# Three projection columns taken half by half, and layer 1's tables stored from ACT's queue

## The chip, the cores and the metric

The kernel runs on one core of one Trainium2 chip. The metric is the device time of one execution in microseconds (us). The engines of the core are TensorE (PE, with its weight loads as PEld), VectorE (DVE), ScalarE (ACT), GpSimd (POOL) and SyncE (SP). Each executes its own instruction list strictly in order. SP, ACT and POOL can also issue DMAs, and a DMA waits at its place in the list of the engine that issues it.

## The reference

A two-layer encoder on x of 1024 tokens by 1024 channels, in float32. Cut to what matters:

```python
for l in range(2):
    u = x @ w_in[l]                       # 1024 -> 2048: 16 columns of 128 channels
    conv, hyena, s5, q, k, v = split(u)   # 4 mixer groups of 256 channels
    # q, k: RMS norm per head, 2-D rotary (rope), then attention with 4 query and 2 key heads
    # hyena: 3-tap conv, then two long convolutions, by spectra of filters made from a small MLP
    # s5: linear state space, run both ways with tables made from lambda, B, C
    # conv: a * sigmoid(gate), 31 taps, layer norm, silu
    x = layernorm(ALPHA * x + concat(rms(each group)) @ w_out[l])
    x = layernorm(ALPHA * x + moe(x))     # 16 experts, each takes 128 tokens, SwiGLU
```

The hyena spectra and the s5 tables of a layer depend on weights alone, not on x.

## The kernel before, in words

**Projection.** `mixer(l)` loads the rows of the layer, normalises them (layer 1) and transposes them on PE into two resident tiles, `hTh` (high part) and `hTl` (rest). Each of 16 columns of `w_in` is then taken by `col(ct, evac)` (L1043): two PSUM tiles (one per half of the tokens), two weight loads `wr` of half a column on SP's queue, the cast `wh` on ACT (L1053), the rest `wl` on POOL (L1054), and 48 matmuls of 128x128 by 128x512: 8 blocks of the contraction, 2 halves, 3 products. A half needs only the transposed rows of its own 512 tokens. 16 columns are 768 matmuls a layer. The parts run in the order `qkv` (columns 12 to 15), `gated`, `chunks`, `hyrows` in layer 0, and `qkv`, `hyrows`, `gated`, `chunks` in layer 1. In `qkv` columns 12 to 14 are evacuated into `uq`, transposed into `rx`, and put through `rope` (L760 to L790) on DVE and POOL; column 15 goes to `VD`.

**The side work.** `s5_setup` and `spectra` make the tables of a layer. For layer 0 they run beside layer 0's projection (`side` in `mixer`), all of them emitted ahead of the parts (`step(side, 40)`). The four quarters of `s5_setup` compute `Q` and `R` (in a buffer with the tag `M`) on POOL, `M` on DVE, transposes of `M` and products `Q,Bb` on PE, and `Kp` on DVE, which empties the PSUM of `Q,Bb` (L589 to L592). `spectra` makes four `gf` and four `Z` (the DVE functions `stage1` and `fly`, L275 to L307). For layer 1 both run beside layer 0's experts (`experts`, L1420), where `Q` and `R` are on DVE too.

**Experts.** Weights stream in as `er`; ACT casts `eh` (L1460), DVE subtracts `el` (L1463), PE multiplies; POOL gathers each expert's rows (`xs`, L1488) and scatters the result (`accD`, L1538).

**What sets the order.** The code is emitted once; a list scheduler of the build with a time model then fixes each engine's instruction list. PSUM has pairs of banks with names; `ps(tag)` looks up which bank names a tag may use and takes them in turn. A tag that is not listed falls back to `acc` (L172), and in layer 0's mixer that is so for the tag `su` of `s5_setup`. Tiles of one bank name are handed out in the order in which they are emitted, two at a time.

Of the kernel before, what the change touches and what calls it, by code (L numbers as in the profile page):

```python
# [11 lines left out]
F32 = mybir.dt.float32  # L12
F32R = mybir.dt.float32r
# [123 lines left out]
class Trunk:  # L137
# [178 lines left out]
    def spectra(self, l, side, HD, after=None):  # L316

        nc, I = self.nc, self.I
        with self.pool("sh", 1, side) as hp:
            hid = hp.tile([128, 512], F32, tag="hid2", name=self.name("hid"))  # L320
            with self.pool("ml", 1, side) as mp:
# [8 lines left out]
                for s, dst in enumerate((h1, hid)):  # L330
                    arg = mp.tile([128, 512], F32, tag="harg", name=self.name("arg"))
                    red = mp.tile([128, 512], F32, tag="hred", name=self.name("red"))
                    p = self.ps(tag="hy")
                    for h in range(2):
                        r = slice(64 * h, 64 * h + 64)
# [8 lines left out]
            with self.pool("sp", 1, side) as sp:  # L344
                dft_s = self.const("dft_s", [128, 8, 128], pool=sp)
                w3r = I["hw3"][l].rearrange("p (o s f c) -> p o s f c", o=2, s=2, f=2)
                for f in range(2):
                    c = slice(128 * f, 128 * f + 128)
                    win = sp.tile([128, 8, 128], F32, tag="win", name=self.name("win"))
                    nc.sync.dma_start(win, I["hy_win"][:, :, c])  # L350
                    for o in range(2):
                        w3 = sp.tile([128, 2, 128], F32, tag="w3", name=self.name("w3"))
                        nc.sync.dma_start(w3, w3r[:, o, :, f])
                        hb = sp.tile([1, 128], F32, tag="hb", name=self.name("hb"))
                        nc.sync.dma_start(hb, I["hbias"][l, o:o + 1, c])
                        gf = sp.tile([128, 8, 2, 128], F32, tag="gf", bufs=2 if l else 1, name=self.name("gf"))
                        for i in range(0, 8, 2):
                            p = self.ps((128, 2, 2, 128), tag="hy")
                            for j in range(2):
                                r = slice(64 * (i // 4), 64 * (i // 4) + 64)  # L360
                                n = 128 * ((i + j) % 4)
                                self.mm(p[:, j], hid[r, n:n + 128], w3[r], True, True)
                            nc.vector.tensor_mul(gf[:, i:i + 2], p, win[:, i:i + 2, None].to_broadcast([128, 2, 2, 128]))
                        nc.vector.memset(gf[0:1, 0, 1], 0.0)
                        nc.vector.tensor_add(gf[0:1, 0, 0], gf[0:1, 0, 0], hb)
                        yield

                        def emit(p, r):
                            q = (8 - r) % 8
                            self.mm(p[:, 0, :], self.dft_f[:, r, 0, :], gf[:, r, 0, :], True, False)  # L370
                            self.mm(p[:, 0, :], self.dft_f[:, q, 0, :], gf[:, q, 1, :], False, True)
                            self.mm(p[:, 1, :], self.dft_f[:, r, 1, :], gf[:, r, 0, :], True, False)
                            self.mm(p[:, 1, :], dft_s[:, q, :], gf[:, q, 1, :], False, True)

                        A = sp.tile([128, 4, 2, 128], F32, tag="A", name=self.name("A"))
                        B = sp.tile([128, 4, 2, 128], F32, tag="B", name=self.name("B"))
                        self.stage1(sp, emit, A, B, 128)
                        if l:
                            yield
                        Z = sp.tile([128, 8, 2, 128], F32, tag="gf", bufs=2 if l else 1, name=self.name("Z"))  # L380
                        self.fly(sp, A, B, Z, 128)
                        yield
                        (nc.sync if l == 0 else nc.gpsimd).dma_start(HD[o, f], Z)
                        yield


# [2 lines left out]
    def s5_setup(self, l, side, dram, after=None, between=()):  # L389
        nc, I = self.nc, self.I  # L390
        SD, KD, rD = dram
        v = nc.vector
        gp = nc.gpsimd
        q_ = nc.sync if l == 0 else gp
        with self.pool("s5q", 1, side) as keep, ExitStack() as work:
            sp = work.enter_context(self.pool("s5p", 1, side))

# [80 lines left out]
            u = t([2, 16], "u8")  # L478
# [56 lines left out]
            for q in range(4):  # L535
# [30 lines left out]
                for k in range(2):  # L566
                    p = self.ps((128, 4, 128), tag="su")
# [6 lines left out]
                hi = [tables[1][:, c, gs, :, None].to_broadcast([128] + sh) for c in range(2)]  # L574
                lo = [tables[0][:, c, gs, None, :].to_broadcast([128] + sh) for c in range(2)]
# [4 lines left out]
                for gi in range(4):  # L580
                    g = 4 * q + gi
                    for d in range(2):
                        o = pk[d][32 * gi:32 * gi + 32]
                        h = slice(64 * d, 64 * d + 64)
                        w = slice(2 * d, 2 * d + 8)
# [411 lines left out]
    def mixer(self, l, setup, st):  # L997
# [5 lines left out]
        with ExitStack() as ph:  # L1003
# [43 lines left out]
            def col(ct, evac):  # L1047
                ps = [self.ps(tag="col") for _ in range(2)]
                for k0 in (0, 4):
                    raw, wh, wl = [ww.tile([128, 4, 128], t, tag=n, bufs=b, name=self.name(n))  # L1050
                                   for t, n, b in zip((F32, F32R, F32R), ("wr", "wh", "wl"), (2, 2, 4))]
                    nc.sync.dma_start(raw, I["w_in"][l, ct, :, k0:k0 + 4])
                    nc.scalar.copy(wh, raw)  # L1053
                    nc.gpsimd.tensor_sub(wl, raw, wh.bitcast(F32))  # L1054
                    for f in range(2):
                        r = slice(512 * f, 512 * f + 512)
                        for k in range(4):
                            self.mm3(ps[f], wh[:, k, :], wl[:, k, :], hi[:, k0 + k, r], lo[:, k0 + k, r], k0 + k == 0, k0 + k == 7)
                for f in range(2):
                    evac(f, ps[f].rearrange("p (i n) -> p i n", n=128))  # L1060

            def rows(a, f):
                u = wp.tile([128, 10, 128], F32, tag="hyu", bufs=2, name=self.name("hyu"))
                col(4 + 2 * a + f, lambda f, p: nc.scalar.copy(u[:, 1 + 4 * f:5 + 4 * f], p))
                v.memset(u[:, 0, 0:1], 0.0)
                v.memset(u[:, 9, 127:128], 0.0)
                v.tensor_copy(u[:, 0, 1:128], u[:, 8, 0:127])
                v.tensor_copy(u[:, 9, 0:127], u[:, 1, 1:128])
                d = hz.tile([128, 8, 128], F32, tag="hx" if a else "hz", bufs=4 if a else 2, name=self.name("hx"))
                self.hyena_short(l, u, sw, 2 * a + f, d, wp)  # L1070
                xs.append(d)
# [16 lines left out]
                    step(n0, 1)  # L1088

            def qkv():  # L1090
                for c in range(4):
                    u = wp.tile([128, 8, 128], F32, tag="hyu", bufs=2, name=self.name("uq"))
                    col(12 + c, lambda f, p: nc.scalar.copy(u[:, 4 * f:4 * f + 4], p))
                    x = a0.tile([128, 8, 128], F32, tag="aQ100" if c % 2 else "aQ202", name=self.name("rx"))
                    for i0 in (0, 4):
                        p = self.ps((128, 4, 128), tag="tp")
                        for i in range(4):
                            self.tr(p[:, i, :], u[:, i0 + i, :])
                        nc.scalar.copy(x[:, i0:i0 + 4], p)
                    if c < 3:  # L1100
                        self.rope(c, x, tab, gn[:, c // 2], RD, a0)
                    else:
                        nc.sync.dma_start(VD, x)
                    yield
                ready.append(1)
# [435 lines left out]
    def run(self, depth=DEPTH):  # L1541
        nc, tc = self.nc, self.tc
        self.rt = self.ctx.enter_context(tc.tile_pool(name="rt", bufs=1))
        setup = self.setup(0)
        for l in range(depth):
            self.psum(mm="mm", hy="hy", tp="tp", cv="cv", tx="cv tp", acc="acc", col="mm")
            with ExitStack() as st:
                mg, ws, hz = self.mixer(l, setup, st)
                self.psum(mm="mm acc", tp="tp cv", tx="tp cv", acc="hy")
                lg = self.project(l, mg, ws, hz)  # L1550
            sl = self.route(l, lg)
            self.psum(mm="mm acc", tp="tp", tx="tp", hy="cv", su="hy")
            side = iter(())
            if l + 1 < depth:
                setup = self.setup(l + 1)
                side = chain(self.s5_setup(l + 1, "right", setup[1]), self.spectra(l + 1, "right", setup[0]))
            self.experts(l, sl, side, *((5, 4) if l + 1 < depth else (10, 0)))
            for _ in side:
                pass
        with self.pool("fin", 2) as pool:  # L1560
            dst = self.out.rearrange("(n i) d -> i n d", i=8)
            for i, h in enumerate(self.rows_in(depth, pool, 2, 4)):
                nc.scalar.dma_start(dst[i], h)
# [20 lines left out]
```

## Time and profile before

| | |
|---|---|
| three runs | 2885.1, 2892.15, 2893.3 us, median 2892.15 us |
| the profiled execution | 2887.34 us, span 2885.2 us |
| granted TensorE clock, mean | 0.917 |
| busy in the span | PE 85%, DVE 79%, ACT 46%, POOL 20% |
| layer 0's projection | ends at about 346 us of the span |
| layer 0's experts | about 855 to 1533 us |
| layer 1's projection | about 1558 to 1831 us |

The span is that of one execution taken by the profiler; its own time is 2.1 us longer, and it lies 4.8 us under the median. "Busy" counts compute instructions, not waits, and is an average over stages with different limits.

### The profile page before, as it was taken

To read this page: it belongs to the slowest core of one execution; us is meant where nothing else is said; L and a number is where in the kernel's file an instruction comes from. 1 tells how busy PE (TensorE), PEld (TensorE's weight loads), DVE (VectorE), ACT (ScalarE), POOL (GpSimd) and SP (SyncE) were. 2 spreads that over 40 slices of the span, in tenths; PEclk is the share of its full clock that TensorE was granted. 3 is DMA by queue.
4 is the path that set the end of the run, shared out by engine and by line. 5 is a ranking of instruction groups with operands and counts; after the bars stand their busy time and mean duration, and the time that the engine had idled before them with its cause. 6 is when DMAs were issued, how large, how long until landed. Compare 5 with 4: busy or idle time off the path is not lost.

```text
span 2885.2 us, 32858 instructions
## 1 busy us (share of the span) xinstructions
PE 2461.9 (85%) x12054; PEld 1911.1 (66%) x12054; DVE 2271.7 (79%) x3635; ACT 1321.6 (46%) x1471; POOL 574.5 (20%) x376
## 2 busy tenths in 40 slices
PE   3889968879949978999994999789995899999992
PEld 2668734657738756778883787456684788777781
DVE  8984877677659989998886578687666799888886
ACT  2212313333128755666662332323411677766772
POOL 2663110312021022210102422112201111111101
PEclk9999968889969998999996999889897899999996
DMA  5143240333448988999984321632336699999993
GB/s 191 62 156 129 59 106 1 76 86 114 161 182 317 362 301 287 371 358 347 338 295 158 109 63 63 114 64 63 105 118 264 238 390 392 357 359 361 371 335 142
DMA packets 238961, 603.51 MB, mean 209 GB/s; under 512 B 50598, under 2 KB 97934, under 8 KB 236496
## 3 DMA queue, kind: packets, MB, share of 16 engines
q1 hardware_dynamic: 216720, 524.28, 51.2%
q0 software_dynamic: 13184, 46.72, 6.1%
q10 hardware_dynamic: 8896, 30.42, 2.7%
q8 instruction: 95, 1.56, 0.2%
q14 instruction: 66, 0.54, 0.1%
HBM read 520.99 MB, written 80.33 MB: 208 GB/s over the span
## 4 chain that ended last, share of the span: by engine, by line
PE 55%; DVE 22%; issue 10%; DMA 7%; ACT 3%; POOL 3%; SPq 1%; DVEq 0%; ACTq 0%; POOLq 0%
PE ps L181 52%; PE ps L189 3%; DVE el L1463 3%; DMA accD<-hid,ix 1%; DVE amx L824 1%; ACT eh L1460 1%; DVE s5z L656 1%; DVE junk L1399 1%; DMA T<-KD 1%; DMA c_edge<-in_edge 1%; DVE hrow L244 1%; DVE s5z L655 1%; DMA wr<-in_w_out 1%; DMA SD<-M 1%; DVE st L218 0%
## 5 line engine op out<-in xcount | busy, mean ns | idle before, releaser
L181 PE MATMUL ps<-eh,xh 128*128 128x512 f32 x3072 | 971.9, 397 | 5.7 <-ACT xh L254 3.6
L1463 DVE TENSOR_TENSOR el<-er,eh 128x2048 fp32r<-128x2048 f32 x378 | 859.0, 2287 | 90.9 <-ACT eh L1460 87.7
L1460 ACT CAST eh<-er 128x2048 fp32r<-128x2048 f32 x384 | 730.3, 1913 | 241.3 <-PE ps L181 219.9
L181 PEld LDWEIGHTS ps<-eh,xh 128*128 128x128 f32 x3072 | 576.6, 190 | 124.4 <-ACT xh L254 5.4
L181 PE MATMUL ps<-el,xh 128*128 128x512 f32 x1536 | 612.0, 403 | 49.7 <-DVE el L1463 49.3
L181 PEld LDWEIGHTS ps<-el,xh 128*128 128x128 f32 x1536 | 291.1, 190 | 132.6 <-DVE el L1463 70.4
L1538 POOL DMA_INDIRECT accD<-hid,ix x32 | 88.5, 2765 | 895.3 <-ACT hid L1537 858.3
L181 PE MATMUL ps<-aQ,aQ 128*128 128x512 f32 (+2 forms) x384 | 185.2, 552 | 65.3 <-DVE amx L824 30.8
L181 PE MATMUL ps<-hTh,wh 128*128 128x512 f32 x512 | 209.7, 410 | 6.4 <-DVE gate L1118 4.4
L181 PE MATMUL ps<-hTl,wh 128*128 128x512 f32 x512 | 207.4, 405 | 0.3 <-DVE hTl L255 0.3
L181 PE MATMUL ps<-hTh,wl 128*128 128x512 f32 x512 | 202.2, 400 | 4.9 <-POOL wl L1054 4.9
L181 PE MATMUL ps<-wo,mg 128*128 128x512 f32 x768 | 195.3, 408 | 5.3 <-ACT wo L1275 3.1
L181 PEld LDWEIGHTS ps<-aQ,aQ 128*128 128x128 f32 (+2 forms) x384 | 74.3, 208 | 150.1 <-DVE amx L824 53.0
L181 PEld LDWEIGHTS ps<-wo,mg 128*128 128x128 f32 x768 | 144.3, 194 | 39.8 <-ACT wo L1275 3.9
L254 ACT CAST xh<-ps 128x512 fp32r<-128x512 f32 x128 | 74.8, 584 | 188.0 <-PE ps L189 187.8
L1054 POOL TENSOR_TENSOR wl<-wr,wh 128x512 fp32r<-128x512 f32 x64 | 92.8, 1452 | 241.1 <-ACT wh L1053 237.8
L181 PE MATMUL ps<-aP,aV 128*96 128x512 f32 x256 | 137.9, 633 | 2.1 <-ACT aP L851 2.1
L181 PEld LDWEIGHTS ps<-hTh,wh 128*128 128x128 f32 x512 | 98.4, 192 | 34.0 <-issue 5.8
L181 PEld LDWEIGHTS ps<-hTh,wl 128*128 128x128 f32 x512 | 98.4, 192 | 27.1 <-POOL wl L1054 6.1
L1053 ACT CAST wh<-wr 128x512 fp32r<-128x512 f32 x64 | 39.6, 620 | 166.4 <-PE ps L181 122.3
L181 PEld LDWEIGHTS ps<-hTl,wh 128*128 128x128 f32 x512 | 98.6, 193 | 23.3 <-issue 3.8
L851 ACT ACTIVATE aP<-ps 128x512 f32<-128x512 f32 x128 | 73.8, 596 | 82.8 <-PE ps L181 77.2
(461 smaller groups left out, 3737.7 us busy)
## 6 DMA issues: line engine op xcount, KB each, us to landing
er<-in_wg SPq DMA_DIRECT2D x128, 1024.0 KB, 8.1
er<-in_wu SPq DMA_DIRECT2D x128, 1024.0 KB, 9.4
er<-in_wd SPq DMA_DIRECT2D x128, 1024.0 KB, 6.5
wr<-in_w_in SPq DMA_DIRECT2D x64, 256.0 KB, 3.0
S<-SD SPq DMA_DIRECT2D x16, 768.0 KB, 4.7
hD<-hrow ACTq DMA_DIRECT2D x16, 512.0 KB, 3.2
H<-HD SPq DMA_DIRECT2D x8, 1024.0 KB, 4.8
wr<-in_w_out SPq DMA_DIRECT2D x16, 512.0 KB, 3.2
```

What stands on the lines that cost most here:

```text
L181: self.nc.tensor.matmul(ps, l, r, start=start, stop=stop)
L189: self.nc.tensor.transpose(out, in_, self.ident)
L244: nc.vector.tensor_add(y, y, b)
L254: nc.scalar.copy(h, p)
L655: v.tensor_tensor_scan(zf[:64, 1:512], wf[:64, 0:511], xf[:64, 0:511], 0.0, op0=OP.mult, op1=OP.add)
L656: v.tensor_tensor_scan(zf[64:, 510::-1], wf[64:, :0:-1], xf[64:, :0:-1], 0.0, op0=OP.mult, op1=OP.add)
L851: nc.scalar.activation(P[:, h], p, AF.Exp)
L1053: nc.scalar.copy(wh, raw)
L1054: nc.gpsimd.tensor_sub(wl, raw, wh.bitcast(F32))
L1460: nc.scalar.copy(h, raw)
L1463: (nc.gpsimd if used[0] <= 3 else v).tensor_sub(lo, raw, h.bitcast(F32))
L1538: nc.gpsimd.indirect_dma_start(out=self.accD, out_offset=bass.IndirectOffsetOnAxis(ap=ix[:, 0:1], axis=0), in_=y, in_offset=None, compute_ ...
```

## The change

A new `cols()` takes columns 12, 13 and 14 together: all six weight loads, casts and subtractions first, then the first half of the tokens for the three columns, then the second half. Its six PSUM tiles have a tag of their own, `cols`, which takes the bank names `mm` and `acc` in turn. The high weights of the three columns and the first one's `wl` lie in tiles of `rope` and attention (`aQ101`, `aQ102`, `aQ200`, `aQ201`), and the third column's result in the buffer `hsy`. Column 15 goes by `col` as before. The rest of the edit moves the stores of layer 1's tables (`HD`, `SD`, `KD`, `rD`, and the load of `s5lam`) from POOL's queue to ACT's; layer 0's stay on SP's.

```diff
-                        (nc.sync if l == 0 else nc.gpsimd).dma_start(HD[o, f], Z)
+                        (nc.sync if l == 0 else nc.scalar).dma_start(HD[o, f], Z)
...
-        q_ = nc.sync if l == 0 else gp
+        q_ = nc.sync if l == 0 else nc.scalar
...
+            def cols(cts, us):
+
+                ws = []
+                for n, ct in enumerate(cts):
+                    h = a0.tile([128, 8, 128], F32R, tag=("aQ101", "aQ102", "aQ200")[n], name=self.name("wh"))
+                    w = a0.tile([128, 8, 128], F32R, tag="aQ201", name=self.name("wl")) if n == 0 else None
+                    for k0 in (0, 4):
+                        raw = ww.tile([128, 4, 128], F32, tag="wr", bufs=2, name=self.name("wr"))
+                        lw = w[:, k0:k0 + 4] if n == 0 else ww.tile([128, 4, 128], F32R, tag="wl", bufs=4, name=self.name("wl"))
+                        nc.sync.dma_start(raw, I["w_in"][l, ct, :, k0:k0 + 4])
+                        nc.scalar.copy(h[:, k0:k0 + 4], raw)
+                        nc.gpsimd.tensor_sub(lw, raw, h[:, k0:k0 + 4].bitcast(F32))
+                        ws.append((h[:, k0:k0 + 4], lw))
+                for f in range(2):
+                    r = slice(512 * f, 512 * f + 512)
+                    for n, u in enumerate(us):
+                        p = self.ps(tag="cols")
+                        for k in range(8):
+                            h, w = ws[2 * n + k // 4]
+                            self.mm3(p, h[:, k % 4], w[:, k % 4], hi[:, k, r], lo[:, k, r], k == 0, k == 7)
+                        nc.scalar.copy(u[:, 4 * f:4 * f + 4], p.rearrange("p (i n) -> p i n", n=128))
+
...
             def qkv():
+                us = [wp.tile([128, 8, 128], F32, tag=t, bufs=b, name=self.name("uq"))
+                      for t, b in (("hyu", 2), ("hyu", 2), ("hsy", 1))]
+                cols((12, 13, 14), us)
                 for c in range(4):
-                    u = wp.tile([128, 8, 128], F32, tag="hyu", bufs=2, name=self.name("uq"))
-                    col(12 + c, lambda f, p: nc.scalar.copy(u[:, 4 * f:4 * f + 4], p))
+                    if c < 3:
+                        u = us[c]
+                    else:
+                        u = wp.tile([128, 8, 128], F32, tag="hyu", bufs=2, name=self.name("uq"))
+                        col(12 + c, lambda f, p: nc.scalar.copy(u[:, 4 * f:4 * f + 4], p))
...
-            self.psum(mm="mm", hy="hy", tp="tp", cv="cv", tx="cv tp", acc="acc", col="mm")
+            self.psum(mm="mm", hy="hy", tp="tp", cv="cv", tx="cv tp", acc="acc", col="mm", cols="mm acc")
```

The six tiles of `cols` in layer 0 are, in the order of their emission, ps_1547 (first half, column 12, bank mm), ps_1573 (column 13, acc), ps_1599 (column 14, mm), and for the second half ps_1625 (12, acc), ps_1651 (13, mm), ps_1677 (14, acc). The s5 tables' PSUM tiles, from ps_870 to ps_1482, are emitted before them and lie in acc too.

PE of the kernel before in layer 0, just where the side work's first matmuls stand (ps_1628 and ps_1739 are columns of the projection, `w,hid` is the first step of a `gf`, `uq` a transpose ahead of a rope):

```order
117 L181 MATMUL ps_1628<-hTh_94,wl_1661 128x512
118 L181 MATMUL ps_852<-w_213_847,hid_778 128x256 x2
119 L181 MATMUL ps_856<-w_213_847,hid_778 128x256 x2
120 L189 MATMUL ps_1692<-c_ident,uq_1626 128x128 x4
121 L181 MATMUL ps_1739<-hTh_94,wh_1742 128x512
122 L181 MATMUL ps_1739<-hTl_95,wh_1742 128x512
```

PE of the changed kernel at the place where the side's first matmul stands (ps_1651 is column 13's second half, ps_1848 two matmuls of column 15):

```order
92 L181 MATMUL ps_1651<-hTh_94,wl_1532 128x512
93 L189 MATMUL ps_1704<-c_ident,uq_1512 128x128 x4
94 L181 MATMUL ps_1848<-hTh_94,wh_1850 128x512
95 L181 MATMUL ps_1848<-hTl_95,wh_1850 128x512
96 L181 MATMUL ps_852<-w_213_847,hid_778 128x256 x2
97 L181 MATMUL ps_856<-w_213_847,hid_778 128x256 x2
98 L181 MATMUL ps_860<-w_213_847,hid_778 128x256 x2
99 L181 MATMUL ps_864<-w_213_847,hid_778 128x256 x2
100 L181 MATMUL ps_893<-gf_851,c_dft_f 128x128 x3
```

Before, the side's matmuls stand between columns, two or three at a time. In the changed list everything from row 96 to row 205 belongs to the side work (the `gf` of three spectra, the transposes of `M`, all `Q,Bb`), with no column matmul between; ahead of row 96 stand 76 column matmuls (24 each of ps_1547, ps_1599 and ps_1651, and 4 of column 15).

PE of the kernel before at the end of the fourth quarter's `Q,Bb` (ps_1481 and ps_1482; ps_2124 is a column of a later part):

```order
494 L181 MATMUL ps_1481<-Q_1451,Bb_520 32x128 x2
495 L181 MATMUL ps_1482<-Q_1451,Bb_520 32x128 x2
496 L181 MATMUL ps_1266<-w_306_1261,hid_778 128x256 x2
497 L181 MATMUL ps_1481<-Q_1451,Bb_520 32x128 x2
498 L181 MATMUL ps_1482<-Q_1451,Bb_520 32x128 x2
499 L181 MATMUL ps_2124<-hTh_94,wh_2157 128x512
500 L181 MATMUL ps_2124<-hTl_95,wh_2157 128x512
501 L181 MATMUL ps_2124<-hTh_94,wl_2158 128x512
```

PE of the changed kernel at the end of the same quarter:

```order
203 L181 MATMUL ps_1482<-Q_1451,Bb_520 32x128 x2
204 L181 MATMUL ps_1481<-Q_1451,Bb_520 32x128 x2
205 L181 MATMUL ps_1482<-Q_1451,Bb_520 32x128 x2
206 L181 MATMUL ps_1573<-hTh_94,wh_1525 128x512
207 L181 MATMUL ps_1573<-hTl_95,wh_1525 128x512
208 L181 MATMUL ps_1573<-hTh_94,wl_1527 128x512
```

The fourth quarter was followed by one of the last columns; now it is followed by ps_1573, the first half of column 13, whose bank is one that ps_1481 held.

POOL of the kernel before in layer 0's experts, at the stores of the first quarter (`accD` is a scatter, `xs` a gather):

```order
171 L1538 DMA accD<-hid_8074,ix_7373 1024x1024
172 L1488 DMA xs_8422<-h1D,ix_8418 128x1040
173 L597 DMA SD_6423<-Q_7649 128x4x128
174 L595 DMA SD_6423<-S_7566 128x1024
175 L597 DMA SD_6423<-Q_7649 128x4x128
176 L598 DMA SD_6423<-M_7670 128x1024
177 L600 DMA KD_6424<-Kp_7900 16x240 x4
```

ACT of the changed kernel at the same stores:

```order
536 L595 DMA SD_6419<-S_7562 128x1024
537 L1488 CAST eh_8465<-er_8463 128x2048
538 L1565 ACTIVATE hid_8070<-ps_8323,xs_7373 128x512
539 L597 DMA SD_6419<-Q_7645 128x4x128
540 L1565 ACTIVATE hid_8070<-ps_8324,xs_7373 128x512
541 L1488 CAST eh_8483<-er_8481 128x2048
542 L597 DMA SD_6419<-Q_7645 128x4x128
543 L1488 CAST eh_8501<-er_8499 128x2048
544 L1488 CAST eh_8548<-er_8546 128x2048
545 L1488 CAST eh_8566<-er_8564 128x2048
546 L598 DMA SD_6419<-M_7666 128x1024
```

The stores stood in one row behind a scatter and a gather; now they stand singly between the casts `eh` and the activations `hid`.

## Rows read from the trace of the kernel before

**Rows 1.** The page, the chain that ended last, by engine.

```profile
PE 55%; DVE 22%; issue 10%; DMA 7%; ACT 3%; POOL 3%; SPq 1%; DVEq 0%; ACTq 0%; POOLq 0%
```

**Rows 2.** Busy time by stretch: stretch, its length, then engines as headed.

```profile
core 0: us, PE busy (x) PEld busy (x) DVE busy (x) ACT busy (x) POOL busy (x), PEclk, DMA share, GB/s
...
100.00:198.00 98.00, 79.97 (x451) 63.53 (x449) 89.26 (x134) 20.74 (x36) 75.51 (x54) 0.91 0.29 96
198.00:346.00 148.00, 146.50 (x810) 120.26 (x811) 86.77 (x169) 41.40 (x72) 51.72 (x38) 1.00 0.35 114
```

**Rows 3.** PE, matmuls on hTh alone: stretch, length, busy (count), clock, DMA.

```profile
40.00:80.00 40.00, 12.69 (x32) 0.91 0.31 114
80.00:198.00 118.00, 57.50 (x169) 0.93 0.30 96
```

**Rows 4.** The same for the matmuls on hTl.

```profile
40.00:80.00 40.00, 8.01 (x16) 0.91 0.31 114
80.00:198.00 118.00, 35.55 (x85) 0.93 0.30 96
```

**Rows 5.** PE's timeline at the projection's end: start, length, instruction, count.

```profile
343.49 1.73 PE L181 MATMUL ps<-Z,c_dft_i 128*128 128x128 f32 x14
...
345.92 0.40 PE L181 MATMUL ps<-hTl,wh 128*128 128x512 f32 x1
...
346.84 0.40 PE L181 MATMUL ps<-hTh,wl 128*128 128x512 f32 x1
```

**Rows 6.** PE's groups from 198 to 346 us: count, busy, mean ns, idle before.

```profile
L181 PE MATMUL ps<-gf,c_dft_f 128*128 128x128 f32 x96 | 13.3, 275 | 0.0
L181 PE MATMUL ps<-w,hid 64*128 64x256 f32 x24 | 6.2, 393 | 0.0
...
L181 PE MATMUL ps<-Q,Bb 64*32 64x128 f32 x64 | 2.4, 276 | 0.0
```

**Rows 7.** POOL's timeline: the last instruction of the fourth quarter's Q.

```profile
219.71 1.56 POOL L551 TENSOR_TENSOR Q<-Q,bgw 128x640 f32<-128x640 f32 x1
```

**Rows 8.** DVE's timeline: the last instruction of the third fly.

```profile
235.98 0.68 DVE L294 SCALAR_TENSOR_TENSOR Z<-flx,flw 128x512 f32<-128x512 f32 x1
```

**Rows 9.** DVE's groups from 72 to 198 us, two of rope's nine.

```profile
L780 DVE TENSOR_TENSOR rr<-rx,c_rope 128x256 f32<-128x256 f32 x6 | 7.5, 1252 | 1.1 <-POOL rx L774 1.1
...
L786 DVE TENSOR_TENSOR rr<-rr,rr 128x512 f32<-128x512 f32 x3 | 2.1, 695 | 0.0
```

**Rows 10.** Busy time from 1000 to 1200 us, columns as in Rows 2.

```profile
1000.00:1200.00 200.00, 166.57 (x841) 127.20 (x841) 184.27 (x221) 114.81 (x90) 54.44 (x40) 0.93 0.88 315
```

**Rows 11.** DVE's waits from 1000 to 1200 us: total, times, longest.

```profile
DVE Q L546 <- DMA SD<-Q: 10.1, 1, 10.1
DVE M L546 <- DMA SD<-M: 5.2, 1, 5.2
```

**Rows 12.** POOL's timeline at the first stores of layer 1's tables.

```profile
1055.39 9.17 POOL L1538 DMA_INDIRECT accD<-hid,ix  x1 [39.64 <-ACT hid L1537]
1064.87 2.49 POOL L1488 DMA_INDIRECT xs<-h1D,ix  x1 [0.30 <-issue]
1067.35 0.86 POOL L597 DMA_DIRECT2D SD<-Q  x1
```

**Rows 13.** DVE's timeline: the last instruction of the Q stored there.

```profile
1057.67 0.82 DVE L551 TENSOR_TENSOR Q<-Q,bgw 128x640 f32<-128x640 f32 x1
```

**Rows 14.** ACT's casts of the experts, 900 to 1533 us: busy, then idle before.

```profile
L1460 ACT CAST eh<-er 128x2048 fp32r<-128x2048 f32 x174 | 331.5, 1911 | 159.6 <-PE ps L181 151.5 <-DMA er<-in_wg 2.8 <-DMA er<-in_wd 2.7
```

**Rows 15.** SP's timeline: two kinds of table stores of layer 0.

```profile
163.47 0.39 SPq L597 DMA_DIRECT2D SD<-Q  x1
...
179.64 1.71 SPq L600 DMA_DIRECT2D KD<-Kp  x4
```

**Rows 16.** Busy time at the start of layer 1's projection, columns as in Rows 2.

```profile
1558.00:1584.00 26.00, 14.09 (x50) 10.55 (x51) 22.80 (x38) 9.62 (x13) 11.24 (x4) 0.52 0.44 162
1584.00:1600.00 16.00, 14.30 (x76) 11.10 (x75) 7.63 (x12) 6.81 (x12) 2.59 (x2) 1.00 0.38 148
```

## The prediction

> **What bounds the kernel now.** I read the chain that ended last first. PE makes up 55% of it and DVE 22% [rows 1], so no single engine is the limit and the answer has to be read stage by stage. The change touches three stages: layer 0's projection, layer 0's experts (where layer 1's tables are stored) and layer 1's projection.
>
> In layer 0's projection I read the busy time by stretch. From 100 to 198 us PE works 80 of 98 us while DVE works 89 and POOL 76: the side work, which goes back and forth between DVE, POOL and PE, is the slow part, and PE fills its waits with columns. From 198 to 346 us PE is busy for 146.5 of 148 us and DVE for 87 [rows 2]. So the projection ends at 346 us because PE ran out of time: from 198 us each PE microsecond that was missed earlier is paid in full. The number to carry is how many of the 768 column matmuls are done by 198 us. A block of the contraction takes three matmuls, two on hTh and one on hTl; the counts are 32 and 16 up to 80 us, then 169 and 85 [rows 3, 4], together 302. Some 254 of them ran in the shade of the side work.
>
> In the experts I read DVE first. Between 1000 and 1200 us it is busy for 184 us of 200 and PE for 167, at a granted clock of 0.93 [rows 10]; its waits there are 10.1 us for a store of `Q` and 5.2 us for a store of `M`, from single buffers [rows 11]. In layer 1's projection PE is idle at the start, 11.9 of 26 us and then 1.7 of 16, the first stretch at a granted clock of 0.52, between the levels of 1.2 and 2.4 GHz [rows 16].
>
> **Layer 0's projection: the loss.** The edit removes no matmul. It gives three of the six `cols` tiles the bank name `acc`, and in layer 0 the tables' PSUM tiles are in `acc` too and were emitted earlier. ps_1573, the first of the three, must therefore wait for the bank of the fourth quarter's `Q,Bb`. Being an in-order engine, PE then has nothing else to do beside the side work: its list holds 76 column matmuls, then the whole of the tables' matmuls, then the other 692. The shade in which 254 columns ran is largely lost.
>
> When do columns start again? Call it T. Two things must be done: the fourth `Q` on POOL, which ended at 219.7 + 1.6 = 221.3 us [rows 7], and the `Kp` copies on DVE, which now stand behind the third fly, which ended at 236.7 us [rows 8]. Both came that late because rope shared DVE with them. Rope now stands behind the side on DVE. Nine groups of it, from 7.5 us down to 2.1 us, sum to 39.9 us, all before 198 us [rows 9]; without them the fourth `Q` could end at about 181 us and the fly at about 197 us. POOL loses rope's products and most `wl` from that stretch as well. I take T = 190 us, between the two, and keep 170 us (DVE with hardly a wait: of its 89 us of work from 100 to 198 us some 40 are rope, but the last two fly and quarters still follow) and 200 us as ends.
>
> From T on PE is full, as it was from 198 us. The end of the projection is then T, plus the 148.4 us from 198 us to the end, plus the columns that are late, minus the side's matmuls that are now early. Late are 302 - 76 = 226 columns at 0.23 us (four starts from 345.92 to 346.84 us [rows 5]): 52.0 us. Of the side, before ran 96 `gf,c_dft_f` from 198 us, with a third as many of the other kind, so 128 in all; the last spectrum's 64 stay behind T, 64 come before it. At 1.73 / 14 = 0.124 us each [rows 5] that is 7.9 us. With 20 of the 24 `w,hid` (2.5 to 5 us, so 3) and `Q,Bb` and the rest (3 us) [rows 6] some 14 us are early. Transposes of `uq`, 28 of them that were done by 198 us, come later: 3.5 us. The end is T + 148.4 + 52.0 - 14 + 3.5 = T + 190, so 380 us for T = 190, against 346.4: a loss of 33.6 us. The gates' multiplies on DVE are queued behind the three ropes now, and PE waits for their banks; DVE had 61 us free from 198 us [rows 2], so I add only 2 us (0 to 8). Sum: **+35 us**, with +14 for T = 170 and +52 for T = 200 with 8 us of gates. Behind the projection the order of work is that of before, so I find nothing that gives this back.
>
> **Layer 0's experts: the gain.** The first `Q` of this kind was complete on DVE at 1058.5 us [rows 13]. POOL was then in a scatter that took 9.2 us and a gather of 2.5 us, and issued the store at 1067.35 us [rows 12], 8.9 us late; DVE waited for its landing later. On ACT's list the same stores stand behind one or two casts. So at most the 15.3 us of the two waits go away, and DVE, the busiest engine there, can use nearly all of it. I take 10 us, as the landing itself remains and ACT can hold a store up behind a cast that waits for PE. What the stores cost ACT: four quarters of four to SD at 0.39 us and a fourfold one to KD at 1.71 us [rows 15], 4 x 3.3 = 13 us, and 3 us for those to HD and the rest at the same price: 16 us, against 151.5 us in which its casts wait for PE [rows 14]. That cover hides them. Without it, the 16 us less the 10 would be a loss of 6 us. The upper end of the gain is PE's whole idle time from 1000 to 1200 us, 33 us [rows 10]. Sum: **-10 us** (-33 to +6).
>
> The Trainium skill, in DMA: Bandwidth & Descriptors, section Issuing engines are not separate DMA queues, speaks against this part: DMAs of any engine share the same 16 DMA engines, and another issuing engine saves only the sequencer's time of starting them. By that rule the gain here would be near nothing and the sum +33 us. The trace has the DMA share at 0.88 there, which agrees with it, and the 8.9 us behind a scatter, which do not: that is issue time, and not small.
>
> **Layer 1's projection.** Here the tables are elsewhere and `acc` is free, so the three first halves, 72 matmuls in place of 24, can fill gaps while the last rows are normalised. The first rows bound the gain: 1.7 us idle from 1584 to 1600 us [rows 16], and part of the stretch before, where the rows of the first half are not all there yet. I take 4 us. Against it the first rope starts later, since column 12 is complete after 96 column matmuls and no longer after 48: 48 x 0.23 = 11 us, by which DVE's work moves towards the end of a stretch that PE bounds; I take 2 us of it, and the 8 us of the bad end if most of it shows. Sum: **-2 us** (-6 to +8).
>
> **Sum.** 35 - 10 - 2 = +23 us on the profiled 2887.3 us: 2910 us. From the median of the three runs it would be 2915 us; they spread over 8 us, and 0.3% of the time, 8.7 us, is about what a measurement can tell from no change. I say 2911 us.
>
> **Rivals.** *The experts gain nothing* (0.2): ACT's waits for PE stand right ahead of the stores, or the transfers themselves are what DVE waited for. For it: ACT's 151.5 us of waiting. Against it: the stores' 8.9 us behind the scatter. Time: 2887.3 + 35 - 2 = 2920 us, up to 2926 us if 6 us of ACT's time show. The rule on shared DMA engines ends here.
>
> *The experts' idle time comes back whole and the block is short* (0.12, the other side): one long stall of DVE leaves PE cold and the following experts late, so curing it could return up to all 33 us; with T at 170 us the loss is 14 us, and the sum 14 - 33 - 2 = -21: 2866 us. It decides against my forecast once the gain in the experts exceeds the block's cost less 2 us; with T at 176 us and half of the 33 us it is about even.
>
> *Little is seen* (0.13): T near 170 us and the two waits gone: 14 - 15 - 2 = -3 us, 2884 us, or, if the halves do not let PE start earlier in layer 1 and the gain is 10, 2891 us. Rope's 40 us off DVE would have to speed up the side to DVE's bare work, but it also waits for POOL, PE and landings.
>
> **How the numbers follow.** The forecast, a loss of 9 to 38 us, has 0.55; rivals 0.2, 0.12 and 0.13. Its own range is 2897 to 2926 us. Leaving out the far ends of the first two rivals, 8 in 10 lie between 2884 and 2936 us. Faster by over 0.3% means under 2883 us: the second rival and nothing else, 0.12. Within 0.3%: the third rival and little of the forecast, 0.14. Slower: 0.74.
>
> **What would show each step.** In the changed profile: from some 80 to 190 us PE is far from full, with hardly a column matmul, and the granted clock falls; the first matmul of ps on hTh after that is released by DVE's `Kp` near 190 us; PE is then full to about 380 us. In the experts the DVE waits for SD stores shrink from 15.3 us to under 6, and ACT shows table stores of under 1 us. Layer 1's projection starts as before and ends within a few us of its old length. Wrong I would be above all if T were 170 us or less, or if the later stages hide the late end of the projection, for which I see no cover.

## The result, and the profile after

The changed kernel takes 2934.4 us (median of 4 runs, 2932.9 to 2940.1) against 2888.7 us: a ratio of 1.0169 with a 95% interval of 1.0156 to 1.0183, slower by 46 us in the medians and by 47.5 us in the two profiled spans. The forecast was slower by 23 us, 2911 us; the time lies inside the range, near its upper end, and the change is twice the one forecast.

To see where it went, four landmarks of the traces: the start of the last column matmul of layer 0's projection, the first gather and the last scatter of layer 0's experts, and the first gather of layer 1's. Each row below is the time between two of them, in us.

| stretch | before | after | difference | forecast |
|---|---|---|---|---|
| start to end of layer 0's projection | 346.8 | 392.9 | +46.1 | +35 |
| rest of layer 0's mixer, to the first gather | 495.3 | 497.9 | +2.6 | 0 |
| experts of layer 0, first gather to last scatter | 692.1 | 675.9 | -16.2 | -10 |
| last scatter to first gather of layer 1 | 705.2 | 720.8 | +15.6 | -2 |
| rest | 645.8 | 645.2 | -0.6 | 0 |

A second trace of the kernel before gives 346.9, 495.7, 694.5, 699.6 and 645.9, so the first three agree within 3 us and the fourth within 6.

Busy time by stretch of the changed kernel, columns as in [rows 2]; the last row is the stretch of [rows 10], moved by 48.7 us:

```profile
100.00:198.00 98.00, 48.67 (x359) 39.30 (x357) 74.42 (x117) 8.57 (x19) 64.56 (x48) 0.72 0.26 91
198.00:346.00 148.00, 144.06 (x672) 119.16 (x673) 57.81 (x120) 36.63 (x60) 46.16 (x36) 0.97 0.30 97
346.00:393.00 47.00, 47.00 (x245) 38.37 (x245) 38.92 (x72) 17.90 (x30) 11.25 (x7) 1.00 0.20 62
1048.70:1248.70 200.00, 177.17 (x913) 135.88 (x912) 197.72 (x234) 123.82 (x97) 50.12 (x10) 0.97 0.96 337
```

From 100 to 198 us PE works 49 of 98 us in place of 80, at a granted clock of 0.72 in place of 0.91. The next view, PE's matmuls on hTh alone, says which work is missing (columns as in [rows 3]):

```profile
40.00:100.00 60.00, 18.52 (x50) 0.86 0.33 111
100.00:198.00 98.00, 0.00 (x0) 0.72 0.26 91
198.00:346.00 148.00, 117.17 (x361) 0.97 0.30 97
346.00:394.00 48.00, 33.96 (x102) 1.00 0.20 60
```

Between 100 and 198 us there is not one column matmul. What PE waited for from 60 to 300 us (total, times, longest; the four longest), and the timelines of DVE and of PE where the block ends:

```profile
PE ps L181 <- DVE gf L363: 19.2, 3, 17.2
PE ps L189 <- DVE M L550: 11.7, 1, 11.7
PE ps L181 <- DVE Kp L589: 9.7, 1, 9.7
PE ps L181 <- DVE gate L1146: 3.8, 2, 3.4
```

```profile
197.04 0.68 DVE L294 SCALAR_TENSOR_TENSOR Z<-flx,flw 128x512 f32<-128x512 f32 x1
197.65 0.27 DVE L590 COPY Kp<-ps 128x112 f32<-128x112 f32 x1
197.83 0.28 DVE L589 COPY Kp<-ps 128x128 f32<-128x128 f32 x1
```

```profile
187.78 0.71 PE L181 MATMUL ps<-Q,Bb 64*32 64x128 f32 x28 [0.74 <-POOL Q L551]
198.17 0.80 PE L181 MATMUL ps<-hTh,wh 128*128 128x512 f32 x1 [9.67 <-DVE Kp L589]
```

With no column in its list, PE waits for the side work's own steps. The fourth `Q` is ready at 187.7 us and the last `Q,Bb` follow at once. The third fly ends at 197.7 us, the `Kp` copies that empty the bank stand behind it, and the wait of 9.7 us for `Kp` is the one that ends with the first column matmul, at 198.2 us. From there PE is almost full again (191 of 195 us); its last column matmul:

```profile
392.92 0.40 PE L181 MATMUL ps<-hTh,wl 128*128 128x512 f32 x1
```

From 900 to 1600 us DVE's longest waits are these (the second lies behind the last scatter, at the start of layer 1); the two of [rows 11], 10.1 and 5.2 us for stores of the tables, are no longer among its waits:

```profile
DVE el L1491 <- ACT eh L1488: 34.9, 45, 2.9
DVE st L218 <- DMA hrow<-accD: 15.3, 1, 15.3
DVE xh L255 <- ACT xh L254: 6.0, 3, 2.9
```

### The profile page after: what moved, and what is told of

Its sections match the earlier page's. It is cut to its first block, busy times and chain, and to the rows that moved or that the text cites. A ratio compares the mean times of both kernels' runs of the same rounds, so it can differ in the third digit from the quotient of the medians.

```text
span 2932.7 us, 32810 instructions
## 1 busy us (share of the span) xinstructions
PE 2482.2 (85%) x12054; PEld 1928.4 (66%) x12054; DVE 2265.7 (77%) x3635; ACT 1321.6 (45%) x1471; POOL 572.3 (20%) x338
## 4 chain that ended last, share of the span: by engine, by line
PE 54%; DVE 26%; issue 8%; DMA 7%; ACT 3%; POOL 1%; SPq 1%; DVEq 0%; ACTq 0%; POOLq 0%
PE ps L181 51%; DVE el L1491 5%; PE ps L189 3%; ACT eh L1488 1%; DMA accD<-hid,ix 1%; DVE amx L824 1%; DVE hrow L244 1%; DVE junk L1427 1%; DVE s5z L656 1%; DMA T<-KD 1%; DVE s5z L655 1%; DMA c_edge<-in_edge 1%; DMA wr<-in_w_out 1%; DVE st L218 0%; DMA er<-in_wg 0%
## 5 line engine op out<-in xcount | busy, mean ns | idle before, releaser
L1566 POOL DMA_INDIRECT accD<-hid,ix x32 | 105.9, 3310 | 1039.6 <-ACT hid L1565 966.2
L1054 POOL TENSOR_TENSOR wl<-wr,wh 128x512 fp32r<-128x512 f32 x52 | 74.9, 1440 | 250.6 <-ACT wh L1053 199.7
L255 DVE TENSOR_TENSOR xh<-ps,xh 128x512 fp32r<-128x512 f32 x128 | 87.6, 684 | 26.5 <-ACT xh L254 26.5
```

Of the source, the lines that this page charges most:

```text
L255: nc.vector.tensor_sub(lo[:, k:k + 4, i * 128:(i + 1) * 128], p, h.bitcast(F32))
L1566: nc.gpsimd.indirect_dma_start(out=self.accD, out_offset=bass.IndirectOffsetOnAxis(ap=ix[:, 0:1], axis=0), in_=y, in_offset=None, compute_ ...
```

## The experiments

All start from the kernel before or the changed one; a ratio is that to the kernel before.

**The parts alone.** The first takes only the queue, the second only the columns.

```diff
e1_queue: +                if False:
e1_queue: +                    cols((12, 13, 14), us)
e2_cols:  +        q_ = nc.sync if l == 0 else gp     (and HD on gpsimd)
```

> The stores of layer 1's tables from ACT's queue alone; all columns by col as before. Theory (the queue gives back the 16 us by which the stretch from the first gather to the last scatter of layer 0's experts was shorter in the changed kernel): about 2873 us, with the DVE waits for SD stores (15.3 us before) under 6 us. Rival (the shorter stretch came from the other instruction order, not from the queue): within 8 us of before, and the waits stay.

Measured: 2881.9 us, ratio 0.9985 (0.9974 to 0.9996). From first gather to last scatter it takes 675.9 us, 16 less than before, and no wait of DVE for these stores is left. ACT issues the second store of the first `Q` 0.04 us after DVE has completed it, at 1064.60 us, and DVE's next write into that buffer, at 1074.53 us, has no wait ahead of it. ACT's queue, and then DVE's timeline:

```profile
1063.32 0.38 ACTq L597 DMA_DIRECT2D SD<-Q  x1
...
1064.64 0.38 ACTq L597 DMA_DIRECT2D SD<-Q  x1
```

```profile
1063.80 0.80 DVE L551 TENSOR_TENSOR Q<-Q,bgw 128x640 f32<-128x640 f32 x1
...
1074.53 0.81 DVE L546 TENSOR_TENSOR Q<-Eq,c_s5c 128x640 f32<-128x640 f32 x1
```

The gain in the experts is as in the theory, but 11 us of it are gone elsewhere: the projection ends 1.5 us later, the stretch ahead of the experts takes 500.6 us in place of 495.3, the one behind 707.9 in place of 705.2 or 699.6. The total gain, 5 us in the medians, is a third of the 16 us, and 9 us less than expected.

> The three columns half by half in both layers, the stores left on POOL's queue. Theory (the queue gives 16 us, the columns cost some 46 us in layer 0 and 13 us behind layer 1's projection): about 2950 us, layer 0's projection ends near 393 us. Rival (the queue is worth nothing): about 2934 us.

Measured: 2949.2 us, ratio 1.0216 (1.0199 to 1.0233). The projection ends at 392.7 us and the experts take 695.0 us, with both waits back:

```profile
DVE Q L546 <- DMA SD<-Q: 10.1, 1, 10.1
DVE M L546 <- DMA SD<-M: 6.7, 1, 6.7
```

So between these kernels the queue is worth 16 to 19 us in the experts, and the columns cost the rest.

**The kernel before once more**, for the spread of the landmarks.

> The kernel before once more, for a second trace of it: how much the stretches between landmarks (end of layer 0's projection, first gather, last scatter of layer 0's experts, end of layer 1's projection, first gather of layer 1) differ between two executions of one kernel. Expected: each by under 4 us, and the stretch from layer 1's projection to its first gather near 426 us.

Measured: 2884.8 us, one execution. The differences are 0.1, 0.4, 2.4 and -5.6 us; the last is larger than expected (from layer 1's projection to its first gather 419.5 us), so a difference of 5 us in that stretch says little.

**The bank in layer 0.** Three edits to the banks:

```diff
e5_mm:      cols="mm"                      (the whole change otherwise)
e6_suhy:    cols="mm acc", su="hy"         (the whole change otherwise)
e14_colacc: col="mm" if l else "mm acc"    (the kernel before otherwise)
```

> The whole change, but the tiles of cols take the bank mm alone. Theory (what costs in layer 0 is that three of the six tiles share acc with the tables and so come after all of their matmuls): layer 0's projection ends within 6 us of 347 us and the time is 46 us below the changed kernel, about 2888 us. Rival (the half-by-half order itself starves PE, or the rope that starts later): the projection still ends beyond 375 us, and the time is above 2915 us.

Measured: 2895.3 us, ratio 1.0026 (1.0014 to 1.0037); the last column matmul of layer 0's projection starts at 350.1 us:

```profile
350.09 0.40 PE L181 MATMUL ps<-hTh,wl 128*128 128x512 f32 x1
```

The theory holds for the projection: with the halves and all else left in, its 46 us fall to 3 by taking another bank name. The time is 7 us above the 2888 us expected, since the experts take 685.6 us. DVE waits 10.2 us there for a store of the second `Q`, although ACT issues it. DVE's timeline, here and then in e1_queue at the same write:

```profile
1116.64 0.82 DVE L546 TENSOR_TENSOR Q<-Eq,c_s5c 128x640 f32<-128x640 f32 x1 [10.16 <-DMA SD<-Q]
```

```profile
1108.99 0.80 DVE L546 TENSOR_TENSOR Q<-Eq,c_s5c 128x640 f32<-128x640 f32 x1
```

In e5_mm ACT issued the second half of that store at 1097.73 us, so it took 18.9 us to land; in e1_queue it was issued at 1099.70 us and had landed within 9.3. So here it was the landing that DVE waited for, and the queue is worth only 6.5 us in the experts of this run; why this landing was so long is open.

> The whole change, but the PSUM tiles of the s5 tables go to the bank hy, which the spectra use; mm and acc are then free for cols in layer 0. Theory (the shared bank acc is what stops PE): the projection of layer 0 ends within 6 us of 347 us and the time is that of the whole change with cols in mm, about 2895 us; the tables come later (the last Q,Bb stands behind 624 column matmuls) and nobody waits for them before the s5 part. Rival (the halves, or rope behind the side work, stop PE): the projection still ends beyond 375 us.

Measured: 2905.3 us, ratio 1.0055 (1.0039 to 1.0072). The projection ends at 339.6 us, 7 us before that of the kernel before, but the rest of the mixer takes 518.2 us in place of 495.3, which was not expected. The cause is not shown. A wait for the late tables is not seen: the last store of them is issued at 300.3 us and the first load of the s5 tables at 419.9 us. PE waits more for DVE in attention (`amx`, 32.5 us against 23.9 from 335 to 860 us).

> The kernel before with one edit: in layer 0 the two PSUM tiles of every col take the banks mm and acc in turn. No halves, no common weights, the stores on POOL's queue. 24 column matmuls now stand ahead of the whole of the tables' matmuls (76 in the changed kernel, spread out in the kernel before). Theory (the shared bank alone does it; from the moment T at which columns start again the end is T + 190 us for 76 columns, and 52 x 0.23 = 12 us more for 24): layer 0's projection ends near 400 us (395 to 410), time 2935 to 2950 us. Rival (the halves or the common weights are needed for the loss): the projection ends under 365 us and the time is under 2905 us.

Measured: 2928.5 us, ratio 1.0136 (1.0119 to 1.0152). The shared bank alone does it, with no halves: the projection ends at 379.9 us, 33 us late where the changed kernel is 46 us late. The end is 20 us short of the 400 expected; 14 of them are that columns start at 184 us and not at 198, and the other 6 show how far the sum from T can be off. DVE's timeline shows why: this list has the `Kp` copies ahead of the last part of the third fly, not behind it.

```profile
183.45 0.26 DVE L590 COPY Kp<-ps 128x112 f32<-128x112 f32 x1
183.63 0.28 DVE L589 COPY Kp<-ps 128x128 f32<-128x128 f32 x1
183.83 1.10 DVE L280 TENSOR_TENSOR Z<-flv 128x256 f32<-128x256 f32 x1
```

**Layer 1.** The columns by halves there alone, and then, since rope starts later, rope later by other means:

```diff
e7_q_cols1: +                if l == 1:
e7_q_cols1: +                    cols((12, 13, 14), us)
e10_two:    +                    cols((12, 13), us)             (layer 1 only)
e9_vfirst:  +                for c in ((3, 0, 1, 2) if l else range(4)):
e12_chunks: +            for part in (chunks, qkv, hyrows, gated) if l else ...
e12_chunks: (and the counts of `turn` in layer 1 moved with the parts)
```

> The stores on ACT's queue, the three columns half by half in layer 1 alone (banks mm and acc, where acc is free). Theory (taking the columns by halves in layer 1 starts rope later and costs some 13 us between the end of the projection and the first gather): about 15 us above the kernel with the queue alone. Rival (those 13 us come from another instruction order behind it, by chance, or from layer 0): within 5 us of the kernel with the queue alone, or under it, since the halves fill gaps at the start.

> The stores on ACT's queue, every column by col, but in layer 1 column 15, which needs no rope, ahead of 12, 13 and 14. It delays rope in layer 1 by a column's 48 matmuls (11 us) and by nothing else of the change: no common tiles, no halves, no other bank. Theory (a later rope is what costs in layer 1): 6 to 13 us above the kernel with the queue alone (2882 us), so 2888 to 2895 us. Rival (the cost comes from the buffers that cols shares with rope and attention, or from the halves): within 4 us of 2882 us.

> The stores on ACT's queue, and in layer 1 two columns (12 and 13) half by half in place of three; layer 0 by col. Column 12 is then complete after 72 column matmuls (48 by col, 96 with three). Theory (the cost goes with the delay of rope): between the queue alone (2882 us) and three columns in layer 1 (2894 us), about 2888 us. Rival (a cost of the halves as such): 2894 us as with three.

> The stores on ACT's queue, every column by col, and in layer 1 the two columns of the s5 group ahead of q, k and v, which moves rope back by 96 matmuls, 22 us (three columns by halves moved it by 20 us, column 15 first by 10 us). Nothing of cols is in it. Theory (a rope that is 10 us late is covered, one of 20 us is not): 6 to 16 us above the queue alone, so 2888 to 2898 us. Rival (the cost belongs to the halves and the instruction order that comes with them): within 4 us of 2882 us.

Measured: e7_q_cols1 2894.4 us, ratio 1.0027 (1.0016 to 1.0038); e10_two 2898.1 us, 1.0034 (1.0023 to 1.0045); e9_vfirst 2883.1 us, 0.9987 (0.9978 to 0.9997); e12_chunks 2880.8 us, 0.9969 (0.9957 to 0.9980). The first reduction of rope on DVE in e1_queue, e7_q_cols1 and e12_chunks:

```profile
1597.16 1.22 DVE L770 TENSOR_REDUCE rss<-rr 128x16 f32<-128x1024 f32 x1 [13.09 <-ACT rr L768]
```

```profile
1617.31 1.22 DVE L770 TENSOR_REDUCE rss<-rr 128x16 f32<-128x1024 f32 x1 [22.00 <-ACT rr L768]
```

```profile
1616.02 1.22 DVE L770 TENSOR_REDUCE rss<-rr 128x16 f32<-128x1024 f32 x1 [34.84 <-ACT rr L768]
```

Rope is 20 us later with the halves and 19 us later with the s5 columns first, but only the halves cost 12 us. My theory that a late rope is enough to cost this fell with these runs, and so did its graded form: two columns cost no less than three.

**Which part of cols costs in layer 1.** From the queue alone the parts were added one by one, in layer 1 only: the three columns written ahead of the first rope (e22_ahead); their high weights in the tiles of rope and attention as well (e21_tiles); the loads, casts and subtractions of all three ahead, and column 12's `wl` in such a tile, as well (e20_buffers); the halves and the bank acc as well (e7_q_cols1).

```diff
e22_ahead: +                    for n in range(3):
e22_ahead: +                        col(12 + n, lambda f, p, u=us[n]: nc.scalar.copy(u[:, 4 * f:4 * f + 4], p))
e21_tiles: +                    hh = a0.tile([128, 8, 128], F32R, tag=("aQ101", "aQ102", "aQ200")[n], ...)
e21_tiles: +                        w = ww.tile([128, 4, 128], F32R, tag="wl", bufs=4, ...)
```

> The stores on ACT's queue, and in layer 1 the three columns with all that cols brings but the halves: loads, casts and subtractions of the three ahead, the weights in the tiles of rope and attention, the results in hyu, hyu and hsy; but the matmuls go column by column as in col, in the bank mm. Theory (the halves as such, by the order of work that follows, cost the 12 us of layer 1): within 4 us of the queue alone, 2882 us. Rival (the cost is that of the common tiles and the loads ahead): about 2894 us, as with the halves.

> As the run with the buffers but no halves, with each column's loads, casts and subtractions just ahead of its matmuls in place of all ahead: the stores on ACT's queue, in layer 1 the high weights of three columns in the tiles of rope and attention, the three columns written out ahead of the first rope. Theory (loads and subtractions ahead are what costs): within 4 us of the queue alone, 2882 us. Rival (the common tiles, or the three columns ahead of the first rope): about 2894 us.

> The stores on ACT's queue, and in layer 1 only this of cols: the three columns are written out, each by col with its own weight tiles and bank, ahead of the first rope, their results in hyu, hyu and hsy. Theory (the common tiles cost): within 4 us of 2882 us. Rival (what costs is that all three columns stand ahead of the first rope in the code, so that the list puts rope and all behind it elsewhere): about 2894 us.

| added to the queue alone | median us | ratio, interval | last scatter to first gather |
|---|---|---|---|
| nothing (e1_queue) | 2881.9 | 0.9985 (0.9974 to 0.9996) | 707.9 |
| three columns ahead of rope (e22_ahead) | 2884.2 | 0.9984 (0.9973 to 0.9994) | 709.0 |
| + weights in rope's tiles (e21_tiles) | 2891.8 | 1.0011 (1.0000 to 1.0022) | 723.6 |
| + loads ahead (e20_buffers) | 2894.4 | 1.0022 (1.0013 to 1.0032) | 726.0 |
| + halves, bank acc (e7_q_cols1) | 2894.4 | 1.0027 (1.0016 to 1.0038) | 722.9 |

The step is at the common tiles: 7.5 us in the medians, 14.6 us in the stretch. In all versions with the weights in these tiles the stretch takes 718.9 to 728.9 us (8 traces). Where they are not, 699.6 to 712.3 (8 traces), but for the last kernel below. In layer 1 the halves themselves neither cost nor give anything that these runs can tell.

The edit from e22_ahead to e21_tiles lies in layer 1 alone, and yet the rest of layer 0's mixer takes 494.8 us in place of 503.4. The code of that stretch is the same, and the two traces of the kernel before differ by only 0.4 us there. So a new list by itself can move a stretch by some 8 us, and the 14.6 us cannot be put down to a wait for a tile without seeing that wait.

**The other queue, and the best of both.**

```diff
e8_sp:        +        q_ = nc.sync            (and HD on sync; columns by col)
e16_spchunks: e8_sp with the part order (and `turn`) of e12_chunks
```

> Every column by col; the stores of layer 1's tables on SP's queue, where the weights of the experts are loaded, in place of ACT's. Theory (what the queue gives is that no scatter or gather of POOL stands ahead of the stores): like ACT's queue, 5 us under the kernel before, unless the stores wait for DVE and hold up weight loads behind them; then the time is that of the kernel before or above (2887 to 2900 us).

Measured: 2874.9 us, ratio 0.9952 (0.9935 to 0.9969), the fastest kernel of the study, and 14 us under the kernel before where 5 were expected; the experts take 679.0 us and the stretch behind them 702.3. Issues of the `Q` stores from 1000 to 1250 us, with the median from issue to landing, before, in e1_queue and in e8_sp:

```profile
SD<-Q POOLq DMA_DIRECT2D x8, 256.0 KB, 8.4
```

```profile
SD<-Q ACTq DMA_DIRECT2D x8, 256.0 KB, 12.7
```

```profile
SD<-Q SPq DMA_DIRECT2D x8, 256.0 KB, 6.3
```

The traces tell the landing of seven of the eight stores before, but of only two of the eight in e1_queue and in e8_sp, so these last two medians are rough.

> The two versions that beat the kernel before, together: the stores of layer 1's tables on SP's queue (2875 us alone), and the s5 group's two columns ahead of q, k and v in layer 1 (2881 us with ACT's queue, against 2882 us without). Expected if both are worth what they were: 2870 to 2876 us; if the second is worth nothing, 2875 us.

Measured: 2899.3 us, ratio 1.0041 (1.0029 to 1.0053). Two versions that each beat the kernel before lose together: from the last scatter to the gather it takes 723.2 us, as long as with the common tiles though none are in it. I have no cause for this; it shows that another list can cost as much as those tiles do.

## Why the prediction was right in sign and half in size

Two steps failed: the term for layer 1's projection, which missed by 17.6 us, and the choice of T in layer 0's projection, by 8 us.

*What bounds layer 0's projection* was right: 76 columns ahead, none in the shade of the side work, PE full from T on. *The end is T + 190 us* held: T was 198.2 us, which gives 388 us, the wait for the gates' banks was 3.8 us where I added 2, and the last matmul started at 392.9 us. (In e14_colacc the same sum came out 6 us too high, so part of this closeness is luck.) The step that failed here is *I take T = 190 us, between the two*. The fly, at 236.7 - 40 = 197 us, was the later of two things of which both must be done, and it ended at 197.7 us, 10 us behind the fourth `Q`; a time between the two had no ground. That is 8 of the 11 us by which this term was short. With T near 198 us the two rivals that needed T near 170 us are out. The runs on the banks show that the shared bank is the cause: without it 46 us become 3 or less (e5_mm, e6_suhy), and alone it brings 33 (e14_colacc).

*The gain in the experts* was right in its mechanism and too small: 16 us for 10, just over the 15.3 us of the two waits. The reading that the waits came *from single buffers* was wrong: in layer 1 `Q` and `M` have two buffers each (`bufs=1 + l`), and the wait is that of the third `Q` for the store of the first. Alone, the queue gives 5 us in the end. The 11 us are lost in layer 0's mixer and behind the experts, where the instruction lists are other ones; which of their differences costs was not settled. The rival by which the experts gain nothing is out for the changed kernel, but its condition that the transfer itself is waited for came true in part in e5_mm.

*Layer 1's projection*, 4 us gained and 2 us of it back, is the worst step: -2 forecast, +15.6 in the trace. I priced the matmuls and the time of rope and left out what the diff says in one line, that the weights take the tiles `aQ101`, `aQ102`, `aQ200` and `aQ201`. The sign I gave, that this projection ends within a few us of its old length, came true: from the last scatter to its last column matmul are 282.0 us for 279.7. The other 13 us lie between it and the gather, for which the prediction had no term. My first explanation, that rope is late, does not hold by itself. That the edit which takes the common tiles costs is shown by e22_ahead against e21_tiles. Where the two traces part, counted from the last scatter:

| to | e22_ahead | e21_tiles | difference |
|---|---|---|---|
| rope's first reduction | 78.0 | 89.5 | +11.5 |
| last column matmul | 283.4 | 284.0 | +0.6 |
| last load `T` of the s5 tables | 307.2 | 312.6 | +5.4 |
| last `aQ,aQ` matmul of attention | 521.4 | 531.3 | +9.9 |
| first gather | 709.0 | 723.6 | +14.6 |

```profile
1603.86 1.22 DVE L770 TENSOR_REDUCE rss<-rr 128x16 f32<-128x1024 f32 x1 [18.54 <-ACT rr L768]
```

```profile
1607.82 1.22 DVE L770 TENSOR_REDUCE rss<-rr 128x16 f32<-128x1024 f32 x1 [28.60 <-ACT rr L768]
```

(The last scatter starts at 1525.83 us in the first and at 1518.36 in the second.) The two are level again where PE ends the columns, and part behind them in steps. Whether it is the late rope that comes back there is not shown (in e12_chunks rope was as late without the loss). By which wait it costs is not seen either; PE's waits from 1650 to 2250 us, in the first and in the second:

```profile
PE ps L181 <- ACT aP L851: 9.9, 5, 6.9
...
PE ps L181 <- ACT wo L1306: 3.8, 2, 3.1
```

```profile
PE ps L181 <- ACT aP L851: 12.4, 4, 8.2
PE ps L181 <- ACT wo L1302: 10.4, 2, 8.6
```

PE waits 6.6 us more for the weights `wo` of the output projection and 2.5 us more for `aP` of attention. But in e7_q_cols1 the wait for `wo` is 4.4 us with the same loss, and the kernel before waits 13.7 us for `aP` without it. The lists differ from kernel to kernel, and which entry of a list costs stays open. The three columns by halves with tiles of their own were not run.

The errors add up: +11.1 and +2.6 us in layer 0's mixer, -6.2 in the experts, +17.6 from there to layer 1's gather and -0.6 in the rest make 24.5; with the forecast's 23 that is the 47.5 us of the spans. That the time still fell inside the range owes something to luck: the experts' larger gain took 6 us off the misses.

## What to carry to other kernels

Before work is brought forward, look at whose PSUM bank and whose tiles it takes: a bank shared with a long chain puts an in-order engine behind that whole chain, and the price is what used to run in its shade. Where a restart needs several things done, take the latest of them, not a mean. And where a build-time scheduler makes the lists, add an edit's parts one at a time: two gains need not add, a part that looks free (a tile's name) can be the one that costs, and an edit in one stage can move another by its list alone.

## What the runs showed of the hardware

The 256 KB stores `SD<-Q` did not land sooner from ACT's queue than from POOL's. From POOL the median landing was 6.9 to 8.4 us in the four traces (31 of 32 stores known). From ACT the landings that the traces tell, two of eight in each of eleven, took 6.4 to 17.8 us, and one in e5_mm 18.9 us by DVE's wait. From SP (e8_sp, e16_spchunks; two of eight each) they took 4.6 to 9.1 us, which does not set SP apart from POOL. What ACT's queue improved was the time of issue, not the transfer. This agrees with the half of the Trainium skill's sentence (DMA: Bandwidth & Descriptors, Issuing engines are not separate DMA queues) that only the start is saved, and differs with the other half, that it is small: the store stood 8.9 us behind a scatter and a gather [rows 12, 13], and the stage became 16 us shorter (6.5 us in e5_mm).

Where PE waited on the chain, it also had less clock: from 100 to 198 us, with 49 us of work in 98, the granted clock was 0.72, against 0.91 in the kernel before, with 80 us of work. Both are means between the levels of 1.2 and 2.4 GHz. From 200 to 220 us, where PE was full again, it was still 0.89, and from 346 us on 1.00. What the lower clock cost here was not measured.
